# Score products of the second attention: one float32 product in place of three products of rounded halves

## The chip, the cores and the metric

The kernel runs on one core of one Trainium2 chip. The time is device time in microseconds (us) of one execution, and the figure of a kernel is the median of several executions. Engines are named as in the profile: PE is the matrix engine (PEld its weight loads), DVE the vector engine, ACT the scalar engine, POOL the general one, SP the engine that only issues transfers.

## The reference

Two layers of a decoder trunk on 256 positions of width 2048. Each layer is a token mixer and a gated ConvFFN, each followed by a residual and a layer norm, with shift, scale and gate from a conditioning vector. The mixer of layer 0 is a forgetting attention with 16 heads of width 128. The mixer of layer 1, which is the second attention, is a sliding-window attention (window 128) with 32 query heads of width 64, 4 key and value heads, and a learned sink for each head:

```
s = einsum('bnqhgd,bnkhd->bnhgqk', qb, kb) * (dh ** -0.5)     # dh = 64
p = softmax(concatenate([where(mask, s, -inf), sink], -1))[..., :-1]
o = einsum('bnhgqk,bnkhd->bnqhgd', p, vb)
```

Queries are taken in blocks of 128; a block sees its own 128 keys and the 128 before them. The first block has no keys before it. All inputs, weights and the output are float32.

## The kernel before

**Products.** PE takes float32 operands in two ways here. An operand may be rounded to the type fp32r, and a product of two such operands is one pass. To keep precision, `split` (L82) makes a rounded high half on ACT (L84) and the remainder as a low half on DVE (L85), and a product is then three: high by high, high by low, low by high. An operand left as float32 is multiplied by a plain float32 product instead; the profile shows such a product as two records of PE and two weight loads. The kernel already does so in some places: probabilities by values (`o<-pT,v` in the first attention, `o<-pT,V` in the second) and part of the first attention's output projection (`xs<-w,oW`).

**Weights.** Weights come from memory in blocks, through `stream` (L229). Each block is split by ACT (`wh`, L255) and DVE (`wl`, L259), and PE multiplies it into `ws` or `xs` banks. Of the 14,424 records of PE in the profile, those of the large projections are nearly all.

**The conditioning vectors** are sums of products on DVE (`wa`, L420), spread over the whole program at a rate that the code sets by stage.

**The second attention** is `swa` (L1042). Its input projection is taken in five blocks: keys and values first, then four blocks of queries, one for each group `g` of 8 query heads. Attention work of a group is put, step by step, between the products of later blocks: `later` (L385) queues generators, and `step` takes one step of each after a block of weights has been used. So PE's program has a piece of attention every 3 us or so, between `xs` products.

- `evac_kv` (L1051) rotates the keys on DVE, turns them on PE (`kp`), and splits the turned keys into `kT` high and low, once for each half of the positions and each pair of key heads: 4 splits in all.
- `evac_q` (L1072) scales the queries into `qb` on ACT (L1077), rotates them on DVE (L1035 to L1040), turns them on PE (`qp`, L1085), four transposes at a time, and splits the result into `qT` and `qL`: 8 splits of 128x512 in all.
- `pair` (L1092) handles two heads. The two heads lie in partitions 0 to 63 and 64 to 127 of the turned queries and of the keys (which are stored twice for that), so that the products of a pair are on two halves of the array's rows and go to two banks. For each half of the positions there are three products for each head, 12 products a pair: 6 with 128 columns and 6 with 256. Then come the masked scores and their maximum on DVE (L740), exponentials on ACT (L744), the sums on DVE (L1110 to L1114), the scaling on DVE (L1119) and ACT (L1121), the turning of the probabilities on PE (`T`, L771) with its copy on ACT (`pT`, L773), and the products by values (`o`), again for two heads at once, this time on two halves of the array's columns. There are 16 pairs.

**Order.** The order within an engine is set by the scheduling layer, from the order of the code and what depends on what; each engine then takes its instructions one after another. Tiles of a pool (`gp` has 28 buffers for `gtile`) are reused in turn.

Of the kernel before, what the change touches and what calls it, by code (L numbers as in the profile page):

```python
# [17 lines left out]
P = 128  # L18
# [8 lines left out]
SKV = 4  # L27
# [14 lines left out]
def hybrid_trunk(ctx: ExitStack, tc: tile.TileContext, a: dict, out: bass.AP):  # L42
    nc = tc.nc
    if []:
        ctx.enter_context(tc.manual_schedule(engines={getattr(mybir.EngineType, e) for e in []}))
    f32 = lambda t: t.bitcast(F32)
# [12 lines left out]
    def gtile(name="g"):  # L59
        return gp.tile([P, 2, S], F32R, tag="g", name=name)  # L60

    def ttile(name="t"):
        return tp.tile([P, 2 * S], F32, tag="t", name=name)

    def bank(name="sm"):
        return psp.tile([P, 512], F32, tag="ps", name=name)
# [7 lines left out]
    def mm(o, lhsT, rhs, start=False, stop=False, **kw):  # L74
        return nc.tensor.matmul(o, lhsT, rhs, start=start, stop=stop, **kw)  # L75
# [6 lines left out]
    def split(h, l, src):  # L82

        nc.scalar.copy(h, src)  # L84
        nc.vector.tensor_tensor(l, src, f32(h), op=ALU.subtract)  # L85
# [42 lines left out]
    for j in range(D // WB):  # L128
        ps = bank("cb")
        for i in range(WB // P):  # L130
            k = j * (WB // P) + i
            mm(ps[:, i * P:(i + 1) * P], ident[:KC, k:k + 1].broadcast_to([KC, P]), crow, start=i == 0,
               stop=i == WB // P - 1, skip_group_check=True)
# [52 lines left out]
    def then(fn):  # L186

        work.append(fn)
        if len(work) == 1 and not ahead[0]:
            settle()  # L190
# [23 lines left out]
    def defer(gen):  # L214

        post.append(gen)
# [168 lines left out]
    def later(gens, lag=1):  # L385

        bg["wait"].extend((g, lag) for g in gens)
# [346 lines left out]
    def exps(S_ps, nm, ss, nskc=None):  # L734

        pr = f32(gtile("pr")).rearrange("p a b -> p (a b)")[:, :3 * P]
        for r, (b, e) in enumerate(REGS):

            mk = mask[:, 2:3, :] if r == 0 else (mask[:, 0::2, :] if nskc is None else mask[:, 1:3, :])
            nc.vector.tensor_tensor_reduce(pr[:, b:e].rearrange("p (a k) -> p a k", k=P),  # L740
                                           S_ps[:, b:e].rearrange("p (a k) -> p a k", k=P), mk, -1.0,
                                           -NEG if nskc is None else nskc, ALU.add, ALU.min, nm[:, r:r + 1])
        for r, (b, e) in enumerate(REGS):
            nc.scalar.activation(pr[:, b:e], pr[:, b:e], AF.Exp, bias=nm[:, r:r + 1], scale=-1.0,  # L744
                                 accum_out=ss[:, r:r + 1])
        return pr
# [282 lines left out]
    def rope(t, buf, nh):  # L1029

        t1, t2, t3 = (tp.tile([P, SG, HR], F32, tag=n, bufs=1, name=n)[:, :nh, :] for n in ("r1", "r2", "r3"))
        a1, a2 = buf[:, :, 0:HR], buf[:, :, HR:2 * HR]
        cs = cost[:, t:t + 1, :].broadcast_to([P, nh, HR])
        sn = sint[:, t:t + 1, :].broadcast_to([P, nh, HR])
        nc.vector.tensor_tensor(t1, a1, sn, op=ALU.mult)  # L1035
        nc.vector.tensor_tensor(t2, a2, sn, op=ALU.mult)
        nc.vector.tensor_tensor(t3, a1, cs, op=ALU.mult)
        nc.vector.tensor_tensor(a2, a2, cs, op=ALU.mult)
        nc.vector.tensor_tensor(a1, t3, t2, op=ALU.subtract)
        nc.vector.tensor_tensor(a2, a2, t1, op=ALU.add)  # L1040

    def swa(l, j, edge, after):  # L1042
        w_in, w_o = a["swa_w_in"][j], a["swa_w_o"][j]
        KOFF = SQ * DH2
        kT = [[gtile("kT") for _ in range(SKV // 2)] for _ in range(2)]

        Vg = f32(gtile("V"))
        V = [Vg[:, t, :] for t in range(NT)]
        oT, full = {}, set()

        def evac_kv(t, ps):  # L1051
            kv = ttile("kv")
            nc.scalar.copy(kv, ps)
            kk = kv[:, 0:SKV * DH2].rearrange("p (h d) -> p h d", d=DH2)
            rope(t, kk, SKV)
            kd = ttile("kd")
            kdv = kd.rearrange("p (h u d) -> p h u d", u=2, d=DH2)
            for dup in range(2):
                nc.scalar.copy(kdv[:, :, dup, :], kk)
            yield  # L1060
            v0 = SKV * DH2
            nc.scalar.copy(V[t], kv[:, v0:])
            kp = bank("kp")
            for h in range(SKV):
                nc.tensor.transpose(kp[:, h * P:(h + 1) * P], kd[:, h * P:(h + 1) * P], ident)
            kpv = kp.rearrange("p (h s) -> p h s", s=P)
            yield
            for b in range(SKV // 2):
                split(kT[0][b][:, :, t * P:(t + 1) * P], kT[1][b][:, :, t * P:(t + 1) * P],
                      kpv[:, 2 * b:2 * b + 2, :])  # L1070

        def evac_q(g, ps):  # L1072

            qs_ = []
            for t in range(NT):
                qb = ttile("qb")
                nc.scalar.mul(qb, ps[t], DH2 ** -0.5)  # L1077
                rope(t, qb.rearrange("p (h d) -> p h d", d=DH2), SG)
                qs_.append(qb)
            yield  # L1080
            for n in range(SG // 4):
                qp = bank("qp")
                for j in range(2):
                    for t in range(NT):
                        nc.tensor.transpose(qp[:, (2 * j + t) * P:(2 * j + t + 1) * P],  # L1085
                                            qs_[t][:, (2 * n + j) * P:(2 * n + j + 1) * P], ident)
                th, tl = gtile("qT"), gtile("qL")
                split(th, tl, qp.rearrange("p (j s) -> p j s", j=2))
                later([pair(g, 2 * n + j, (th[:, j, :], tl[:, j, :])) for j in range(2)])
                yield  # L1090

        def pair(g, n, q):  # L1092
            h = g * SG + 2 * n
            qh, ql = q
            kh, kl = (kT[i][g // 2][:, g % 2, :] for i in range(2))
            rows = [slice(i * DH2, (i + 1) * DH2) for i in range(2)]
            sps = [bank("S") for _ in range(2)]
            for r in range(2):
                qs, ks = slice(r * P, (r + 1) * P), slice(0, (r + 1) * P)
                for m, (qx, kx) in enumerate(((qh, kh), (qh, kl), (ql, kh))):  # L1100
                    for o, rr in zip(sps, rows):
                        mm(o[:, r * P:(r + 1) * P + r * P], qx[rr, qs], kx[rr, ks], start=m == 0, stop=m == 2,
                           skip_group_check=True)
            yield
            nm, ss, es = (sp.tile([P, 2, 2], F32, tag=n_, name=n_) for n_ in ("nm", "ss", "es"))
            prs, pTs = [], []
            for i in range(2):
                prs.append(exps(sps[i], nm[:, i, :], ss[:, i, :], nsink[:, h + i:h + i + 1]))
                yield
            nc.vector.tensor_tensor(es, nm, sink[:, h:h + 2].rearrange("p (i o) -> p i o", o=1).broadcast_to([P, 2, 2]),  # L1110
                                    op=ALU.add)
            nc.scalar.activation(es, es, AF.Exp)
            nc.vector.tensor_tensor(ss, ss, es, op=ALU.add)
            nc.vector.reciprocal(ss, ss)  # L1114
            for i in range(2):
                for r, (b, e) in enumerate(REGS):
                    o = prs[i][:, b:e]
                    if r == 0:
                        nc.vector.tensor_scalar_mul(o, o, ss[:, i, r:r + 1])  # L1119
                    else:  # L1120
                        nc.scalar.mul(o, o, ss[:, i, r:r + 1])  # L1121
                yield
            for i in range(2):
                pTs.append(turned(prs[i]))
                yield
            ops = bank("o")
            for b, (d0, s0, s1) in enumerate(AV):
                for rr, pT in zip(rows, pTs):
                    mm(ops[rr, d0:S], V[b][:, g * DH2:(g + 1) * DH2], pT[:, s0:s1],
                       start=b == 0, stop=b == 1, skip_group_check=True)  # L1130
            kc = h // 2
            oT[kc] = o_tile(kc, ops[:, :S], l)
            full.add(kc)

        ps = head_block(w_in, KOFF, after.start)
        then(lambda: ada.update(rate=.1))
        for t in range(NT):
            then(lambda t=t, ps=ps: defer(evac_kv(t, ps[t])))
        then(lambda: (ada.update(rate=0.3), bg.update(gap=2)))
        for g in range(SKV):  # L1140
            if g == 1:
                then(lambda: ada.update(rate=0.33))
            ps = x_stationary(w_in, g * WB, 0, KC, hstat)
            then(lambda g=g, ps=ps: defer(evac_q(g, ps)))
        out_proj(oT, full, w_o, l, edge)
# [104 lines left out]
    for t in range(NT):  # L1250
        mu, rs, _ = moments[t]
# [48 lines left out]
```

## Time and profile before

| | |
|---|---|
| median of 3 executions | 2175.51 us (2174.67 to 2176.22) |
| the profiled execution | 2175.44 us |
| its span, first to last instruction | 2173.7 us |
| mean granted clock of PE | 0.997 |
| PE busy | 2131.2 us, 98% of the span |
| DVE busy | 1741.3 us, 80% |
| ACT busy | 1147.8 us, 53% |
| the second attention's pieces | from 1205 to 1384 us of the span |

The span lies 1.7 us under the execution's own time. In the profile, a product `out<-in` names the moving operand first and the weights second: `S<-kT,qL` has the keys moving over the low halves of the queries. The time of one PE record includes the way through the array, so that records overlap; the pace of PE is read from start to start.

### The profile page before, as it was taken

The numbers are of one execution on the slowest core, as the hardware profiler recorded it, in microseconds if no ns is written. First come the engines' busy times: TensorE is split into PE (matmuls) and PEld (weight loads), VectorE is DVE, ScalarE is ACT, GpSimd is POOL, SyncE is SP. The second block draws the span as 40 slices with busy tenths as digits, with TensorE's granted clock in tenths as the row PEclk, the third lists the DMA queues.
The fourth block names the chain that finished last, engine by engine and source line by source line (L and its number), as shares of the span: only waits on it lengthen the run. The fifth ranks groups of instructions, "written<-read, shape, count | busy, mean of one in ns | idle before, by whom it ended". The sixth has DMA issues, their size and how long they took to land.

```text
span 2173.7 us, 35625 instructions
## 1 busy us (share of the span) xinstructions
PE 2131.2 (98%) x14424; PEld 1917.9 (88%) x14424; DVE 1741.3 (80%) x2391; ACT 1147.8 (53%) x1782; POOL 39.3 (2%) x46
## 2 busy tenths in 40 slices
PE   6999999999999999999999999999999999999997
PEld 6999887579999888999988877789999888999986
DVE  7988898779989988988997897778888555666765
ACT  4546465255575433555555577555555633555541
POOL 1000000010000000000001000010000000000000
PEclk9999999999999999999999999999999999999999
DMA  9998988959888999888885665548777555555552
GB/s 389 420 373 304 373 332 330 369 180 353 316 297 316 337 352 356 321 330 295 323 332 223 246 252 195 184 147 310 271 272 270 194 194 194 194 194 194 194 194 96
DMA packets 89653, 598.59 MB, mean 275 GB/s; under 512 B 10016, under 2 KB 12352, under 8 KB 21136
## 3 DMA queue, kind: packets, MB, share of 16 engines
q1 hardware_dynamic: 89312, 595.87, 74.2%
q8 instruction: 113, 1.85, 0.3%
q0 software_dynamic: 176, 0.44, 0.1%
q14 instruction: 52, 0.43, 0.1%
HBM read 594.18 MB, written 2.10 MB: 274 GB/s over the span
## 4 chain that ended last, share of the span: by engine, by line
issue 56%; PE 39%; DVE 2%; DMA 2%; POOL 1%; ACT 0%; SPq 0%; DVEq 0%; ACTq 0%; POOLq 0%
PE ws L75 25%; PE xs L75 14%; DMA w<-in_fox_w_in_dram 2%; POOL x L693 0%; DVE wa L420 0%; DVE wl L259 0%; PE sm L502 0%; PE lg L75 0%; DVE x L687 0%; POOL rs L667 0%; DVE stats L661 0%; DVE x L659 0%; DVE x L1255 0%; PE sm L539 0%; DVE x L1254 0%
## 5 line engine op out<-in xcount | busy, mean ns | idle before, releaser
L255 ACT CAST wh<-w 128x1024 fp32r<-128x1024 f32 x698 | 733.2, 1053 | 727.0 <-PE ws L75 329.5
L259 DVE TENSOR_TENSOR wl<-w,wh 128x1024 fp32r<-128x1024 f32 x698 | 847.8, 1221 | 327.5 <-ACT wh L255 324.8
L75 PE MATMUL ws<-hH,wh 128*128 128x256 f32 x6400 | 1097.6, 276 | 7.4 <-ACT hH L529 6.7
L75 PEld LDWEIGHTS ws<-hH,wh 128*128 128x128 f32 x6400 | 968.5, 188 | 10.9 <-ACT hH L529 7.1
L75 PE MATMUL ws<-hH,wl 128*128 128x256 f32 x3200 | 879.9, 276 | 2.4 <-DVE wl L259 2.4
L75 PEld LDWEIGHTS ws<-hH,wl 128*128 128x128 f32 x3200 | 601.1, 188 | 3.4 <-DVE wl L259 3.3
L420 DVE CUSTOM_DVE_ANT_0 wa<-wa,cb,acol 128x2048 f32<-128x2048 f32 x192 | 449.4, 2344 | 1.0 <-DMA wa<-in_ada_w_dram 0.7
L75 PE MATMUL xs<-wh,gT 128*128 128x512 f32 x1344 | 414.7, 389 | 0.0
L75 PEld LDWEIGHTS xs<-wh,gT 128*128 128x128 f32 x1344 | 252.3, 188 | 52.3
L75 PE MATMUL xs<-wl,gT 128*128 128x512 f32 x672 | 261.4, 389 | 0.0
L75 PE MATMUL xs<-wh,hH 128*128 128x512 f32 x752 | 253.7, 402 | 3.6 <-ACT wh L255 2.9
L75 PEld LDWEIGHTS xs<-wh,hH 128*128 128x128 f32 x752 | 140.8, 189 | 36.0 <-ACT wh L255 3.5
L75 PE MATMUL xs<-wl,hH 128*128 128x512 f32 x376 | 148.8, 396 | 2.8 <-DVE wl L259 2.8
L75 PEld LDWEIGHTS xs<-wl,gT 128*128 128x128 f32 x672 | 126.2, 188 | 26.0
L1155 ACT ACTIVATE u<-ws,ccol 128x256 f32<-128x256 f32 x176 | 96.8, 562 | 52.6 <-PE ws L75 42.1
L75 PE MATMUL xs<-wh,oT 128*128 128x512 f32 x288 | 96.1, 401 | 1.1 <-ACT wh L255 1.1
L1156 DVE SCALAR_TENSOR_TENSOR u<-ws,ccol,u 128x255 f32<-128x255 f32 x176 | 82.2, 477 | 14.1 <-ACT u L1155 14.1
L75 PEld LDWEIGHTS xs<-wl,hH 128*128 128x128 f32 x376 | 71.0, 189 | 17.4 <-DVE wl L259 3.5
L1158 DVE SCALAR_TENSOR_TENSOR u<-ws,ccol,u 128x254 f32<-128x254 f32 x176 | 83.2, 476 | 2.2
L75 PEld LDWEIGHTS xs<-wh,oT 128*128 128x128 f32 x288 | 53.9, 188 | 13.2 <-ACT wh L255 1.3
L657 DVE TENSOR_TENSOR t<-xs,gate 128x512 f32<-128x512 f32 x48 | 31.5, 684 | 36.6 <-PE xs L75 36.6
L744 ACT ACTIVATE pr<-pr,nm 128x128 f32<-128x128 f32 x96 | 43.3, 452 | 32.0 <-DVE nm L740 31.8
(214 smaller groups left out, 1291.6 us busy)
## 6 DMA issues: line engine op xcount, KB each, us to landing
wa<-in_ada_w_dram SPq DMA_DIRECT2D x192, 1024.0 KB, 6.7
w<-in_ffn_w_up_dram SPq DMA_DIRECT2D x176, 1024.0 KB, 5.4
w<-in_ffn_w_down_dram SPq DMA_DIRECT2D x88, 1024.0 KB, 5.0
w<-in_fox_w_in_dram SPq DMA_DIRECT2D x60, 512.0 KB, 8.6
w<-in_swa_w_in_dram SPq DMA_DIRECT2D x20, 1024.0 KB, 5.8
w<-in_fox_w_in_dram SPq DMA_DIRECT2D x18, 1024.0 KB, 7.5
w<-in_fox_w_o_dram SPq DMA_DIRECT2D x16, 1024.0 KB, 6.9
w<-in_swa_w_o_dram SPq DMA_DIRECT2D x16, 1024.0 KB, 4.9
```

The source lines that it names most:

```text
L75: return nc.tensor.matmul(o, lhsT, rhs, start=start, stop=stop, **kw)
L255: pin(nc.scalar.copy(hp, wp_), False)
L259: nc.vector.tensor_tensor(lp, wp_, f32(hp), op=ALU.subtract)
L420: return nc.vector.tensor_tensor_reduce(w, w, cb, 1.0, acol[:, l, v * KC + k:v * KC + k + 1], ALU.mult, ALU.add, cv[:, k:k + 1])
L657: pin(nc.vector.tensor_tensor(tmp, ps[t], gate[:, d * 512:(d + 1) * 512], op=ALU.mult), end)
L744: nc.scalar.activation(pr[:, b:e], pr[:, b:e], AF.Exp, bias=nm[:, r:r + 1], scale=-1.0, accum_out=ss[:, r:r + 1])
L1155: nc.scalar.activation(u, pf, AF.Identity, bias=cw(CW, f), scale=cw(2, f))
L1156: nc.vector.scalar_tensor_tensor(u[:, 1:], pf[:, :S - 1], cw(1, f), u[:, 1:], op0=ALU.mult, op1=ALU.add)
L1158: nc.vector.scalar_tensor_tensor(u[:, 2:], pf[:, :S - 2], cw(0, f), u[:, 2:], op0=ALU.mult, op1=ALU.add)
```

## The change

The turned keys are copied to one float32 tile for each pair of key heads (2 tiles in place of 4), the turned queries to one float32 tile (in place of `qT` and `qL`), both by a copy on ACT. Each score product is one float32 product. A pair then issues 4 products (2 with 128 columns, 2 with 256) in place of 12.

```diff
-        kT = [[gtile("kT") for _ in range(SKV // 2)] for _ in range(2)]
+        kT = [f32(gtile("kT")) for _ in range(SKV // 2)]
...
             for b in range(SKV // 2):
-                split(kT[0][b][:, :, t * P:(t + 1) * P], kT[1][b][:, :, t * P:(t + 1) * P],
-                      kpv[:, 2 * b:2 * b + 2, :])
+                nc.scalar.copy(kT[b][:, :, t * P:(t + 1) * P], kpv[:, 2 * b:2 * b + 2, :])
...
-                th, tl = gtile("qT"), gtile("qL")
-                split(th, tl, qp.rearrange("p (j s) -> p j s", j=2))
-                later([pair(g, 2 * n + j, (th[:, j, :], tl[:, j, :])) for j in range(2)])
+                qT = f32(gtile("qT"))
+                nc.scalar.copy(qT, qp.rearrange("p (j s) -> p j s", j=2))
+                later([pair(g, 2 * n + j, qT[:, j, :]) for j in range(2)])
...
-            qh, ql = q
-            kh, kl = (kT[i][g // 2][:, g % 2, :] for i in range(2))
+            k = kT[g // 2][:, g % 2, :]
...
-                for m, (qx, kx) in enumerate(((qh, kh), (qh, kl), (ql, kh))):
-                    for o, rr in zip(sps, rows):
-                        mm(o[:, r * P:(r + 1) * P + r * P], qx[rr, qs], kx[rr, ks], start=m == 0, stop=m == 2,
-                           skip_group_check=True)
+                for o, rr in zip(sps, rows):
+                    mm(o[:, r * P:(r + 1) * P + r * P], q[rr, qs], k[rr, ks], start=True, stop=True,
+                       skip_group_check=True)
```

Lines behind the change lie up to three lower in the changed kernel (L1113 becomes L1110, L1119 becomes L1116).

On PE, the first pair (and the `xs` products and query transposes `qp` around it) stands so before:

```order
L75 MATMUL xs<-wl,hH 128x512
L75 MATMUL xs<-wh,hH 128x512
L75 MATMUL S<-kT,qT 128x128 x4
L75 MATMUL S<-kT,qL 128x128 x2
L75 MATMUL S<-kT,qT 128x256 x4
L75 MATMUL S<-kT,qL 128x256 x2
L1085 MATMUL qp<-ident,qb 128x128 x4
```

and so in the changed kernel:

```order
L75 MATMUL xs<-wl,hH 128x512
L75 MATMUL xs<-wh,hH 128x512
L75 MATMUL S<-kT,qT 128x128 x2
L75 MATMUL S<-kT,qT 128x256 x2
L1084 MATMUL qp<-ident,qb 128x128 x4
```

The place among the other products is the same, for all 16 pairs; only the rows of a pair become fewer.

On DVE, at the second pair of the second group (masked scores L740, sums, and the scaling of the probabilities), the order before is:

```order
L740 ISA pr,nm<-S,mask,nsink 128x256
L740 ISA nm 128x1
L1113 TENSOR_TENSOR ss<-ss,es 128x4
L259 TENSOR_TENSOR wl<-w,wh 128x1024
L1114 RECIPROCAL ss<-ss 128x4
L85 TENSOR_TENSOR qL<-qp,qT 128x512
L1119 TENSOR_SCALAR pr<-pr,ss 128x128 x2
L740 ISA pr,nm<-S,mask,nsink 128x128
```

and in the changed kernel:

```order
L740 ISA pr,nm<-S,mask,nsink 128x256
L740 ISA nm 128x1
L1110 TENSOR_TENSOR ss<-ss,es 128x4
L259 TENSOR_TENSOR wl<-w,wh 128x1024
L1111 RECIPROCAL ss<-ss 128x4
L259 TENSOR_TENSOR wl<-w,wh 128x1024
L1116 TENSOR_SCALAR pr<-pr,ss 128x128 x2
L740 ISA pr,nm<-S,mask,nsink 128x128
```

The subtraction `qL` is gone, and a later `wl` subtraction has moved to its place, ahead of the scaling of the probabilities.

## The prediction

> **What bounds the kernel now.** I read the page's table of engines first, then PE's own waits while the second attention runs, then the table by stretches of that stage.
>
> ```profile
> PE 2131.2 (98%) x14424; PEld 1917.9 (88%) x14424; DVE 1741.3 (80%) x2391; ACT 1147.8 (53%) x1782; POOL 39.3 (2%) x46
> ...
> PE S L75 <- DVE qL L85: 2.1, 2, 1.2
> PE qp L1085 <- DVE qb L1040: 1.3, 2, 0.8
> ...
> 1230.00:1265.00 35.00, 33.71 (x191) 26.40 (x190) 34.65 (x85) 23.32 (x51) 0.00 (x0) 1.00 0.73 268
> 1265.00:1300.00 35.00, 33.76 (x209) 25.72 (x208) 29.74 (x91) 26.86 (x71) 0.00 (x0) 1.00 0.68 240
> 1335.00:1370.00 35.00, 34.10 (x206) 25.81 (x205) 25.34 (x78) 25.28 (x69) 0.00 (x0) 1.00 0.47 166
> ```
>
> PE sets the time. In the stretches (width, then busy time of PE, PEld, DVE, ACT, POOL, then clock) PE stands still for 1.3, 1.2 and 0.9 us, at granted clock 1.00. All its waits are on DVE: for low halves of the queries, which the change abolishes, and for rotated queries (`qb`), late because DVE is full (34.65 of 35 us). So two things count: what a pair's scores take on PE, and which waits end.
>
> **The products of a pair.** PE and its weight loads at an undisturbed pair, and PE at a group of products by values:
>
> ```profile
> 1256.34 0.44 PE L75 MATMUL S<-kT,qT 64*128 64x128 f32 x4
> 1256.73 0.45 PE L75 MATMUL S<-kT,qT 64*128 64x256 f32 x4
> 1257.22 0.50 PE L75 MATMUL xs<-wh,hH 128*128 128x512 f32 x1
> ...
> 1256.34 0.30 PEld L75 LDWEIGHTS S<-kT,qT 64*128 64x128 f32 x4 [0.17 <-issue]
> ...
> 1256.90 0.19 PEld L75 LDWEIGHTS S<-kT,qL 64*128 64x128 f32 x2
> ...
> 1260.21 0.87 PE L75 MATMUL o<-pT,V 128*64 128x256 f32 x8
> 1261.01 0.55 PE L771 MATMUL T<-ident,pr 128*128 128x128 f32 x3
> ...
> 369.93 3.60 PE L75 MATMUL xs<-w,oW 128*128 128x512 f32 x8
> 373.36 0.49 PE L771 MATMUL T<-ident,pr 128*128 128x128 f32 x3
> ...
> 1259.66 0.39 PE L75 MATMUL xs<-wl,hH 128*128 128x512 f32 x1
> 1259.89 0.39 PE L75 MATMUL xs<-wh,hH 128*128 128x512 f32 x1
> ```
>
> A pair takes 1257.22 - 1256.34 = 0.88 us from its start to the next work. Its 12 loads go in twos, one for each head (four of them, two such steps, are busy for 0.30, one step and a load of 0.19), the first at 1256.34, the last two at 1256.90. Five steps take 0.56 us, 0.11 each, and the 128-column products (1256.34 to 1256.73 for three steps) keep the same step. So the weight loads pace the group, more than the columns.
>
> A float32 product: eight records with 512 columns take 373.36 - 369.93 = 3.43 us, 0.43 each, and two records make a product, 0.86; a rounded product takes 0.23 (1259.66 to 1259.89). A record moves 512 columns in 0.43, so 256 in 0.215 and 128 in 0.107. A new pair has two records for 128 and two for 256 columns in each head: 2 x 0.107 + 2 x 0.215 = 0.64 us if the two heads run together, as they do now, and 1.29 if one after another. The nearest row is the group by values: the same columns, 2 x (128 + 256) in float32 on two halves of the array. It takes 1261.01 - 1260.21 = 0.80 us, so its halves do run together, with 0.16 for start and end. Its weights have 64 columns, a score's 128. Only the first load lies bare; at 0.11 for 128 columns, 64 more cost 0.055. The rest lie under records of 0.107 or longer. So a pair takes 0.80 + 0.055 = 0.855 us: 16 x (0.855 - 0.88) = **-0.4 us**. Its ends: 0.80 (-1.3 in all), and both heads one after another, 1.29 + 0.16 + 0.055 = 1.50 (+9.9). I take the value near the group by values, a row of float32 halves run together.
>
> The Trainium skill, "FP8 and Floating Point Precision", section TensorE Precision Notes, counts true float32 as four passes through the array, against three for the products removed. The trace agrees on the four (0.86 against 0.23 is 3.7). By passes alone the change would cost PE time; that sum is a rival below, from the rows.
>
> **The waits.** The disturbed places, and an undisturbed one of the query transposes to set against them:
>
> ```profile
> 1266.70 0.44 PE L75 MATMUL S<-kT,qT 64*128 64x128 f32 x4
> 1268.37 0.33 PE L75 MATMUL S<-kT,qL 64*128 64x128 f32 x2 [1.24 <-DVE qL L85]
> 1269.03 0.66 PE L1085 MATMUL qp<-ident,qb 128*128 128x128 f32 x4
> ...
> 1335.75 0.68 PE L75 MATMUL S<-kT,qT 64*128 64x128 f32 x4
> 1337.27 0.33 PE L75 MATMUL S<-kT,qL 64*128 64x128 f32 x2 [0.84 <-DVE qL L85]
> 1337.93 0.66 PE L1085 MATMUL qp<-ident,qb 128*128 128x128 f32 x4
> ...
> 1353.89 0.82 PE L75 MATMUL S<-kT,qT 64*128 64x128 f32 x4
> 1355.16 0.50 PE L75 MATMUL xs<-wh,oT 128*128 128x512 f32 x1
> ...
> 1262.37 0.30 PE L1085 MATMUL qp<-ident,qb 128*128 128x128 f32 x1 [0.81 <-DVE qb L1040]
> 1263.45 0.48 PE L75 MATMUL xs<-wh,hH 128*128 128x512 f32 x1
> ...
> 1297.95 0.55 PE L771 MATMUL T<-ident,pr 128*128 128x128 f32 x3
> 1298.69 0.48 PE L75 MATMUL xs<-wh,hH 128*128 128x512 f32 x1
> ...
> 1234.69 0.68 DVE L85 TENSOR_TENSOR qL<-qp,qT 128x512 fp32r<-128x512 f32 x1
> 1235.29 0.68 DVE L712 SCALAR_TENSOR_TENSOR x<-x,ln 128x512 f32<-128x512 f32 x1
> ...
> 1263.73 0.59 ACT L84 CAST qT<-qp 128x512 fp32r<-128x512 f32 x1
> 1334.89 0.59 ACT L84 CAST qT<-qp 128x512 fp32r<-128x512 f32 x1
> ```
>
> Two pairs stop in their middle for `qL`: 2.33 us (1266.70 to 1269.03) and 2.18 (1335.75 to 1337.93), against 0.88. That is 1.45 + 1.30 = 2.75 us. Their high halves had been ready: `qT` ended at 1264.32 and 1335.48, ahead of the pairs' starts, and the changed pair waits for that copy alone. So **-2.75**. A third pair loses 1.27 - 0.88 = 0.39 (1353.89 to 1355.16) with no `qL` named; I leave it as it is (0), its end is -0.39.
>
> The query transposes from 1262.37 wait for the rotation. From the `T` products at 1261.01 to the next `xs` at 1263.45 are 2.44 us; the same work takes 0.74 at 1297.95. That is 1.70 lost. DVE works without a pause before it, and one `qL` there costs it 0.60 (1234.69 to 1235.29); two lie between 1230 and 1262. So the rotation ends 1.20 earlier, and 0.50 of the wait stays: **-1.20**, with ends 0 and -1.70.
>
> **What may come back.** DVE's order has a `wl` subtraction where `qL` stood, ahead of the scaling. ACT scales the other part of the same probabilities just before `T`:
>
> ```profile
> 1288.96 0.91 ACT L1121 ACTIVATE pr<-pr,ss 128x256 f32<-128x256 f32 x2 [0.50 <-DVE ss L1114]
> 1289.70 0.55 PE L771 MATMUL T<-ident,pr 128*128 128x128 f32 x3
> ...
> L420 DVE CUSTOM_DVE_ANT_0 wa<-wa,cb,acol 128x2048 f32<-128x2048 f32 x12 | 28.1, 2345 | 0.0
> L85 DVE TENSOR_TENSOR qL<-qp,qT 128x512 fp32r<-128x512 f32 x8 | 5.5, 683 | 0.0
> L85 DVE TENSOR_TENSOR kT<-kp,kT 128x256 fp32r<-128x256 f32 x4 | 1.5, 418 | 0.1
> L84 ACT CAST qT<-qp 128x512 fp32r<-128x512 f32 x8 | 4.6, 579 | 0.4 <-PE qp L1085 0.4
> L447 ACT COPY gate<-sm 128x512 f32<-128x512 f32 x2 | 1.2, 586 | 0.0
> ```
>
> The two scalings at 1288.96 take 0.91, the first half of that, to 1289.42; `T` starts at 1289.70, 0.28 later. A PE that comes 3 or 4 us earlier can meet these chains unfinished. The chains also begin on PE and move with it, so most of the gain stays. I allow **+1.0** for new waits, between 0 and 2.34 (one `wa` sum put ahead of a scaling).
>
> At nothing: DVE loses 5.5 + 1.5 = 7.0 us of subtractions, under PE's work apart from the waits counted. ACT's float32 copies cost what its roundings cost (586 against 579 ns for 128x512), on an engine with a third of each stretch idle. Transfers and POOL keep their order. Freed buffers cost nothing, and no wait of PE here names one. If PE's cover went, these 7 us would be a gain that I don't count.
>
> **Sum.** -0.4 - 2.75 - 1.20 + 1.0 = -3.35 us. The span 2173.7 becomes 2170.3; the profiled execution lies 1.74 above its span (2175.44) and 0.07 under the median, so the median becomes 2175.51 - 3.35 = **2172.2 us**, 0.15% less.
>
> **Rivals.**
>
> A. Forecast: heads together, the `qL` waits gone, some waits back: 2172.2, of its own range 2169.4 (-1.3 - 2.75 - 1.70 - 0.39 = -6.1) to 2173.9. Chance 0.66.
>
> B. Slower: float32 products on two halves of the array's rows don't run together. For it: no row here shows float32 on row halves, the group by values uses column halves. Against: rounded products do run together on row halves, and float32 ones on column halves. Price 16 x (1.50 - 0.88) = +9.9, so 2175.51 + 9.9 - 2.75 - 1.20 + 1.0 = 2182.5. It decides once a pair takes over 0.88 + 2.95 / 16 = 1.06 us. Chance 0.12. The Trainium skill, "TensorE: Matmul & The Clock Gate", section Part 3: Packing small matmuls, has products in distinct row groups start some 4 ns apart, naming no type; no run here shows it for float32.
>
> C. The passes decide. Three rounded products of 512 columns take 3 x 0.23 = 0.69, one float32 product 0.86; on a pair's 384 columns the difference is 0.17 x 384 / 512 = 0.13 us, 16 times +2.0 instead of -0.4: 2174.6. Against it, the pair's loads now pace it at 0.11 a step where 128 columns need 0.23 / 4 = 0.06. Chance 0.06.
>
> D. The waits move and don't end: the scaling of the probabilities, behind `wl` and `wa`, stops PE for as long as `qL` did. Then -0.4 alone, 2175.1. For it, 0.28 us of slack at `T`; against it, DVE has 7 us less to do. Chance 0.16.
>
> **How the numbers follow.** The time is A's, 2172.2. The range takes A's lower end and D, and leaves out B: 2169.3 to 2176.0. What a measurement of this kernel can tell from no change is about 0.2%, 4.35 us, so the border is 2171.2. A lies below it with 0.29 of its 0.66 (where less of the waits comes back than allowed): faster 0.29. No change has the other 0.37 of A, C's 0.06 and 0.14 of D: 0.57. Slower has B's 0.12 and 0.02 of D, where more comes back than was gained.
>
> **What would show it.** Right: an undisturbed pair takes 0.85 us with 8 records, the two heads' records starting together; no wait of PE names `qL` or a query copy; the wait of `qp` on `qb` near 1262 shrinks to half a microsecond; DVE's busy time falls by 7 us. Wrong: records of a pair one after another (1.5 us, B), a step that follows the passes (1.0 us, C), or waits of `T`, `qp` or `o` on L1116, L1118 or L1040 that sum to over 2.3 us (D).

## The result and the profile after

The changed kernel takes 2170.15 us, the median of 11 runs, ten of which lie between 2169.84 and 2171.52. The kernel before took 2175.89 beside it (11 runs, 2174.67 to 2177.55). The ratio is 0.9974, with a 95% interval from 0.9966 to 0.9982: 0.26%, or 5.7 us, faster. One of the 11 runs (2374.68 us) and one of ten of the first experiment below (3588.45 us) went at a lower granted clock, 0.851 and 0.558; they move the medians by at most 0.2 us and do not enter the ratios. The prediction was 2172.2 us, 0.15% faster, with "no change" as its likeliest outcome.

The profiled execution of the changed kernel took 2171.03 us, its span 2169.2 (before: 2175.44 and 2173.7). The table of engines:

```profile
PE 2129.6 (98%) x14360; PEld 1914.5 (88%) x14360; DVE 1735.5 (80%) x2379; ACT 1148.8 (53%) x1782; POOL 39.3 (2%) x46
```

PE has 64 records fewer: 16 pairs with 8 in place of 12. PE still sets the time. What changed is how long it stands still in the second attention. The table by stretches (start and end, width, then busy time of PE, PEld, DVE, ACT, POOL, then granted clock, share of the transfers and GB/s), first of the kernel before for the whole stage, which the prediction did not show:

```profile
1205.00:1400.00 195.00, 191.57 (x1079) 149.22 (x1078) 160.47 (x405) 131.41 (x308) 0.00 (x0) 1.00 0.60 213
```

and of the changed kernel, with the same three shorter stretches as in the prediction:

```profile
1230.00:1265.00 35.00, 34.96 (x182) 26.73 (x182) 34.77 (x91) 23.93 (x51) 0.00 (x0) 1.00 0.77 285
1265.00:1300.00 35.00, 35.00 (x205) 26.09 (x205) 31.98 (x98) 27.95 (x76) 0.00 (x0) 1.00 0.71 263
1335.00:1370.00 35.00, 35.00 (x196) 25.88 (x195) 21.08 (x66) 26.00 (x68) 0.00 (x0) 1.00 0.38 136
1205.00:1400.00 195.00, 194.96 (x1039) 149.67 (x1038) 159.30 (x397) 136.71 (x314) 0.00 (x0) 1.00 0.60 222
```

PE's idle time in these 195 us falls from 195 - 191.57 = 3.43 us to 0.04. The list of PE's waits in the stage, two rows before, is empty now. Note that DVE is as full as it was from 1230 to 1265 (34.77 of 35 us): it did not become free, it was merely no longer late at the places where PE needs it.

The pairs and the query transposes on PE in the changed kernel (start, duration, engine, line, operation, count). The first three rows are an undisturbed place; the next are the place of the wait on rotated queries, the two places where a pair stopped for `qL`, and the third disturbed pair:

```profile
1256.79 0.49 PE L771 MATMUL T<-ident,pr 128*128 128x128 f32 x3
1257.21 0.93 PE L75 MATMUL S<-kT,qT 64*128 64x128 f32 x8
1258.06 0.50 PE L75 MATMUL xs<-wh,hH 128*128 128x512 f32 x1
...
1261.81 0.55 PE L771 MATMUL T<-ident,pr 128*128 128x128 f32 x3
1262.19 0.86 PE L1084 MATMUL qp<-ident,qb 128*128 128x128 f32 x4
1262.81 0.48 PE L75 MATMUL xs<-wh,hH 128*128 128x512 f32 x1
...
1266.09 0.93 PE L75 MATMUL S<-kT,qT 64*128 64x128 f32 x8
1266.94 0.66 PE L1084 MATMUL qp<-ident,qb 128*128 128x128 f32 x4
...
1333.17 0.93 PE L75 MATMUL S<-kT,qT 64*128 64x128 f32 x8
1334.02 0.66 PE L1084 MATMUL qp<-ident,qb 128*128 128x128 f32 x4
...
1349.92 0.93 PE L75 MATMUL S<-kT,qT 64*128 64x128 f32 x8
1350.78 0.50 PE L75 MATMUL xs<-wh,oT 128*128 128x512 f32 x1
```

A pair takes 0.85 to 0.86 us from its start to the next work wherever it stands: 1257.21 to 1258.06, 1266.09 to 1266.94, 1333.17 to 1334.02, 1349.92 to 1350.78. (The starts without rounding give 0.855 to 0.857 for all 16; I use 0.856.) The three pairs that took 2.33, 2.18 and 1.27 take that too. In the pair at 1257.21 the records of the two heads start 7 ns apart, four times over (3 to 6 ns for the rounded products before, at 1256.34). From the `T` products to the next `xs`, the place that took 2.44 us takes 1.00 (1261.81 to 1262.81).

Now the stage as a whole. These are the first key transposes and the last pair with the work after it, in the kernel before:

```profile
L1065 PE MATMUL kp<-ident,kd x8: 271/272/276, 1209.6 to 1210.4; 128*128 128x128 f32 x8
...
1362.53 0.44 PE L75 MATMUL S<-kT,qT 64*128 64x128 f32 x4
```

and in the changed kernel:

```profile
L1065 PE MATMUL kp<-ident,kd x8: 271/273/276, 1210.6 to 1211.3; 128*128 128x128 f32 x8
...
1358.11 0.93 PE L75 MATMUL S<-kT,qT 64*128 64x128 f32 x8
```

From the first key transpose to the start of the last pair are 152.9 us before (1209.6 to 1362.53) and 147.5 after (1210.6 to 1358.11): 5.4 us less. What follows the last pair takes as long as before (798.7 and 798.6 us to PE's last record). The span is only 4.5 us shorter, because the changed kernel reached the stage 1.0 us later, through code that the change does not touch. The first 100 us of each, before and after:

```profile
0.00:100.00 100.00, 82.45 (x527) 75.77 (x528) 81.36 (x76) 49.05 (x67) 5.78 (x24) 0.98 0.99 403
```

```profile
0.00:100.00 100.00, 82.10 (x523) 75.53 (x524) 80.51 (x76) 49.17 (x67) 5.78 (x24) 0.93 0.99 401
```

The granted clock was 0.98 in the one execution and 0.93 in the other. That belongs to the execution and not to the kernel, as the last section shows. The medians over many runs differ by 5.7 us, the stage by 5.4.

### The profile page after: what moved, and what is told of

It reads as the page before. It is cut to its first block, busy times and chain, and to the rows that moved or that the text cites. A ratio compares the mean times of both kernels' runs of the same rounds, so it can differ in the third digit from the quotient of the medians.

```text
span 2169.2 us, 35481 instructions
## 1 busy us (share of the span) xinstructions
PE 2129.6 (98%) x14360; PEld 1914.5 (88%) x14360; DVE 1735.5 (80%) x2379; ACT 1148.8 (53%) x1782; POOL 39.3 (2%) x46
## 4 chain that ended last, share of the span: by engine, by line
issue 56%; PE 40%; DVE 2%; DMA 1%; POOL 1%; ACT 0%; SPq 0%; DVEq 0%; ACTq 0%; POOLq 0%
PE ws L75 25%; PE xs L75 14%; DMA w<-in_fox_w_in_dram 1%; DVE wa L420 1%; POOL x L693 0%; DVE wl L259 0%; PE sm L502 0%; PE lg L75 0%; DVE x L687 0%; POOL rs L667 0%; DVE stats L661 0%; DVE x L659 0%; DVE x L1252 0%; PE sm L539 0%; DVE x L1251 0%
```

## The experiments

Two questions were open. First, what was the loss: the waits for the subtractions (PE standing in the middle of a pair), the load of the subtractions on DVE, or the products themselves? Second, why does a float32 pair take 0.856 us: do the heads run together whatever the order of the program, and what sets the pace?

**Is it DVE's load?** This kernel is the changed one with the 12 subtractions put back on DVE; nothing reads their results.

```diff
         kT = [f32(gtile("kT")) for _ in range(SKV // 2)]
+        kL = [gtile("kL") for _ in range(SKV // 2)]
...
+                nc.vector.tensor_tensor(kL[b][:, :, t * P:(t + 1) * P], kpv[:, 2 * b:2 * b + 2, :], hi, op=ALU.subtract)
...
+                nc.vector.tensor_tensor(gtile("qL"), qp.rearrange("p (j s) -> p j s", j=2), qT, op=ALU.subtract)
```

> The changed kernel, with the 12 subtractions of the low halves put back on DVE (8 of 128x512, 4 of 128x256, 7 us in all); nothing reads their results, so PE waits for none of them. Theory W (PE lost its time where it waited for the low halves themselves): the two waits of 1.45 and 1.30 us stay away, a pair takes 0.86 us, and the time is 2175.9 - 0.5 - 2.75 = 2172.6 us or less; the wait of the query transposes for the rotated queries near 1262 us, 1.70 us, is back because DVE is as full as before. Theory L (DVE's load is what held PE up, wherever it was waited for): nearly all waits are back in other places, time 2175 us.

Measured: 2170.85 us, ratio 0.9977 (0.9968 to 0.9987). The subtractions run, and PE has one wait left in the stage:

```profile
L1091 DVE TENSOR_TENSOR qL<-qp,qT x8: 681/684/691, 1235.5 to 1335.7; 128x512 fp32r<-128x512 f32 x8
```

```profile
PE qp L1087 <- DVE qb L1040: 0.4, 1, 0.4
```

All 16 pairs stay at 0.856 us. So DVE can carry the 7.0 us of subtractions (8 x 0.684 and four of the keys) at a price of 0.4 us in the stage (147.9 us from the first key transpose to the start of the last pair, 147.5 in the changed kernel). In the medians it is 0.7 us, less than the width of the interval, and nearly all of the gain stays. The loss was that PE waited for the subtractions, not that DVE made them. The wait on the rotated queries does come back, as the prediction's step for it says, but at 0.4 us and not at 1.70: in this kernel the scheduling has put two `xs` products between `T` and the query transposes and three more behind the first of these, and they cover a part of it. So this run bounds that step and does not measure it.

**Is it the products?** Rounded products again, three for each score, but with no low halves: the queries and keys are rounded once, and the high product is summed three times. The corrections are left out and the scores are three times too large; time alone is read from it.

```diff
-                qT = f32(gtile("qT"))
+                qT = gtile("qT")
...
-                for o, rr in zip(sps, rows):
-                    mm(..., start=True, stop=True, ...)
+                for m in range(3):
+                    for o, rr in zip(sps, rows):
+                        mm(..., start=m == 0, stop=m == 2, ...)
```

> Queries and keys rounded once on ACT, no low halves, and the same high product taken three times, so that PE has the 12 rounded products of the kernel before and DVE no subtraction; the corrections by the low halves are left out. Theory W (the gain comes from waits and DVE's load, the form of the product is worth 16 x 0.03 us): a pair takes 0.88 us, no wait in the stage, time 2170.15 + 0.5 = 2170.6 us. Theory P (the gain comes from the form of the product on PE): nearer to the kernel before, 2174 us or more.

Measured: 2173.47 us, ratio 0.999 (0.9981 to 0.9999), between the two expectations. Undisturbed pairs take 0.88 us, as before the change. But the waits list has two new rows:

```profile
PE S L75 <- DVE oT L85: 1.0, 1, 1.0
PE S L75 <- ACT qT L1087: 0.6, 1, 0.6
```

The first of them on PE, and what DVE did just then:

```profile
1265.32 0.32 PE L75 MATMUL S<-kT,qT 64*128 64x128 f32 x1
1266.63 0.95 PE L75 MATMUL S<-kT,qT 64*128 64x128 f32 x11 [0.99 <-DVE oT L85]
1267.52 0.66 PE L1084 MATMUL qp<-ident,qb 128*128 128x128 f32 x4
...
1263.89 2.35 DVE L259 TENSOR_TENSOR wl<-w,wh 128x1024 fp32r<-128x1024 f32 x2
1266.16 0.41 DVE L85 TENSOR_TENSOR oT<-o,oT 128x256 fp32r<-128x256 f32 x1
```

The scheduling has put two `wl` subtractions (2.35 us) ahead of `oT`, and the pair's second product, the first of the other head, does not start until `oT` has read its source. This pair takes 2.20 us (1265.32 to 1267.52) in place of 0.88. The second row is a wait for a copy of the queries on ACT: from the `T` products at 1300.02 to the pair at 1301.14 are 1.12 us, in the changed kernel 0.42 (1299.21 to 1299.63), so 0.7 is lost. With 16 x (0.88 - 0.856) = 0.4, that is 1.32 + 0.7 + 0.4 = 2.4 of the 2.8 us by which the stage is longer than the changed kernel's. So the run does not separate the two theories cleanly: low halves gone, it still lost PE's time to waits, but to other ones. It shows instead that a new wait of the kind the prediction allowed for (a `wl` or `wa` put ahead of something PE needs) is real; with the other one it costs 2.0 us, within the 0 to 2.34 that were allowed. Such waits come with one order and not with another; the changed kernel's order had none.

**Does the order of the heads matter?** The changed kernel with both products of the first head, then both of the second:

```diff
-            for r in range(2):
-                qs, ks = ...
-                for o, rr in zip(sps, rows):
+            for o, rr in zip(sps, rows):
+                for r in range(2):
+                    qs, ks = ...
```

> The changed kernel with the four products of a pair in another order: both products of the first head, then both of the second, in place of the heads in turn. Orders of the other engines stay. Theory O (PE starts products in the order of its program, and two row halves run together only where products of the two heads alternate): the two heads run nearly one after another, a pair takes 1.3 to 1.5 us in place of 0.86, 16 x 0.45 to 0.65 = 7 to 10 us more, 2177 to 2180 us. Theory I (each half of the rows takes its own products as they come): 0.86 us a pair, 2170.2 us.

Measured: 2170.42 us, ratio 0.9978 (0.9969 to 0.9986). The first pair and the work after it:

```profile
1237.04 0.93 PE L75 MATMUL S<-kT,qT 64*128 64x128 f32 x8
1237.91 0.66 PE L1084 MATMUL qp<-ident,qb 128*128 128x128 f32 x4
```

A pair takes 0.87 us (0.863 without rounding). The two heads run together although the program asks for them one after the other; the theory that the alternation makes them overlap would have cost 7 to 10 us, and falls. The trace shows when records start and not in which order they were issued. That the order did change is read from the edit and from the second head's records, which now start 13 or 14 ns behind the first's in place of 7.

**What is a product worth?** One rounded product for each score (corrections left out, so the scores carry the rounding of queries and keys):

```diff
-                qT = f32(gtile("qT"))
+                qT = gtile("qT")
```

> Queries and keys rounded once, and one rounded product of the high halves for each score block: the corrections by the low halves are left out. PE then has 4 products of one record a pair. By the pace of the weight loads (0.11 us a step, the first one bare) a pair takes 0.16 + 0.11 + 0.10 = 0.37 us in place of 0.86. Theory W with PE as the bound: 16 x 0.49 = 7.8 us less than the changed kernel, 2162.3 us, if the scheduling layer makes no new wait; up to 2165.5 us with waits like the 1.3 and 0.9 us that the run with three high products had. If the engines beside PE set the pace of the stage, most of it is lost: 2168 us or more.

Measured: 2163.66 us, ratio 0.9943 (0.9929 to 0.9956).

```profile
1234.69 0.50 PE L75 MATMUL S<-kT,qT 64*128 64x128 f32 x4
1235.12 0.66 PE L1084 MATMUL qp<-ident,qb 128*128 128x128 f32 x4
```

A pair takes 0.43 us, half a float32 pair's 0.856 and half of the three rounded products' 0.88. So 16 x 0.43 = 6.9 us of PE's work are gone, and the median is 6.7 us under the changed kernel's in the same comparison (2170.4): in this stage PE's time counts one to one. The number also fits a simple account of a pair, though none of its parts was varied alone: four loads take two steps, 0.22 us at 0.11; the other 0.21 are start and end; twelve loads take six steps, 0.66, and again 0.22. The float32 pair fits it by its columns, 0.64, and again 0.22; its eight loads, four steps, would need only 0.44. I expected 0.37 here: start and end were taken too small.

**Was it the place of the wait in the pair?** The kernel before, with the low-by-high products behind all the others. DVE and ACT do the same in the same order. This order does not give the right scores; the products are the same ones, and time alone is read from it.

```diff
-            for r in range(2):
-                qs, ks = ...
-                for m, (qx, kx) in enumerate(((qh, kh), (qh, kl), (ql, kh))):
+            for m, (qx, kx) in enumerate(((qh, kh), (qh, kl), (ql, kh))):
+                for r in range(2):
+                    qs, ks = ...
```

> The kernel before, with a pair's products in another order: high by high and high by low for both halves of the positions first, then low by high for both. The orders of DVE and ACT stay as before. If the two long pairs stop for the low half of the queries, the stop now lies behind eight products in place of four and the pairs take about 2.15 and 2.0 us in place of 2.34 and 2.18, the others 0.88, and the third one, 1.27 us, which names no low half, stays. If they stopped for something else that these products share, the stop stays where it was, behind the first products. 2175 us, no difference that can be timed.

Measured: 2175.03 us in a single run, in the middle of the runs of the kernel before (2174.74 to 2177.54). The three disturbed pairs:

```profile
1266.36 0.72 PE L75 MATMUL S<-kT,qT 64*128 64x128 f32 x8
1268.04 0.50 PE L75 MATMUL S<-kT,qL 64*128 64x128 f32 x4 [0.95 <-DVE qL L85]
1268.46 0.66 PE L1085 MATMUL qp<-ident,qb 128*128 128x128 f32 x4
...
1335.17 1.17 PE L75 MATMUL S<-kT,qT 64*128 64x128 f32 x8
1336.88 0.50 PE L75 MATMUL S<-kT,qL 64*128 64x128 f32 x4 [0.55 <-DVE qL L85]
1337.31 0.66 PE L1085 MATMUL qp<-ident,qb 128*128 128x128 f32 x4
...
1353.24 0.32 PE L75 MATMUL S<-kT,qT 64*128 64x128 f32 x1
1353.89 0.72 PE L75 MATMUL S<-kT,qT 64*128 64x128 f32 x7 [0.33 <-DVE nm L740]
...
1354.78 0.50 PE L75 MATMUL xs<-wh,oT 128*128 128x512 f32 x1
```

The stop moves behind the eight products that need only the high half. From the start of the low-by-high products to the next work are now 0.42 us (1268.04 to 1268.46) and 0.43 (1336.88 to 1337.31); from the same stop it was 0.66 in both pairs before (1268.37 to 1269.03, 1337.27 to 1337.93). The first pair shrinks with that, to 2.10 us in place of 2.33. The second stays near its length (2.14 in place of 2.18), because PE comes to it earlier against DVE: its first eight products now wait 0.26 us on the weight loads for `oT`, a wait that was 0.2 before. The stops follow the low half wherever it is used, so they are waits for `qL` and not for a bank or a weight load.

The third pair is another matter: its stop names the scores of an earlier pair (`nm`, L740) and no low half. I had expected it to stay at 1.27 us; it took 1.54 (1353.24 to 1354.78). Two more pairs, at 1318.11 and 1326.38, took 0.95 and 1.05 with no wait of PE named, which was not expected and is not explained.

**Does the same change pay in the first attention?** There each score sums a rounded product of `A` and `Bm` and three rounded products of queries and keys. The three become one float32 product, beside the same change in the second attention:

```diff
-                th, tl = gtile("qh"), gtile("ql")
+                th = f32(gtile("qh"))
...
-                    split(th, tl, src)
+                    nc.scalar.copy(th, src)
...
-                    mm(o, qh[:, qs], kh[:, ks], skip_group_check=True)
-                    mm(o, qh[:, qs], kl[:, ks], skip_group_check=True)
-                    mm(o, ql[:, qs], kh[:, ks], stop=True, skip_group_check=True)
+                    mm(o, qh[:, qs], kh[:, ks], stop=True, skip_group_check=True)
```

> The changed kernel with the same change in the first attention: turned queries and keys unrounded, one float32 product beside the rounded product that carries the forget terms. DVE loses 32 subtractions there. On PE a head has 2 rounded products and 2 float32 products of two records in place of 8 rounded products; at 0.11 us for a rounded one with its load and 0.107 and 0.215 for a record of 128 and 256 columns that is 2 x 0.11 + 0.64 = 0.86 against 8 x 0.11 = 0.88 us, no difference. Theory W: only waits for these halves can be won, and PE names none of them there, so 2169 to 2170.2 us. Theory L (less load on DVE is worth time where DVE is full): DVE is busy for 259 of 300 us there, 20 us of its work go, and PE's 7 us of idle time in that stretch shrink by some us: 2166 us.

> The change in both attentions once more: 2168.6 us as before, 1.6 us under the changed kernel, if the gain is one of the program and not of one chip; 2170 us if it was chance.

> The changed kernel once more, beside the next one on the same chip: 2170.2 us, 0.9974 of the kernel before.

Measured: 2168.58 us, ratio 0.9965 (0.9953 to 0.9978), and on another chip 2167.09, ratio 0.996 (0.9948 to 0.9973). There the changed kernel itself had 2170.4, ratio 0.9974 (0.9964 to 0.9985). So it is 1.6 and 3.3 us under the changed kernel; the intervals overlap, but it came out under it both times, and it has the lowest medians of the kernels here that drop no correction. One head's scores and the products after it:

```profile
204.39 0.22 PE L75 MATMUL S<-Bm,A 128*128 128x128 f32 x1
...
204.85 0.59 PE L75 MATMUL S<-qh 128*128 128x256 f32 x2
205.09 0.59 PE L75 MATMUL ws<-hH,wh 128*128 128x256 f32 x2
205.51 0.29 PE L75 MATMUL ws<-hH,wl 128*128 128x256 f32 x1
```

The group itself takes 205.09 - 204.39 = 0.70 us in place of 0.91, but the first two `ws` products behind it then take 0.42 (205.09 to 205.51) in place of 0.23: the end of the float32 products lies inside the next work. Group and delay together cost some 0.9 us against 0.91, no real difference. What this stage gained, 2.6 us between the first score and the key transposes of the second attention (1009.15 to 1006.54 us), therefore comes from elsewhere. DVE's busy time in 100 to 400 us fell from 258.95 to 251.18 us, but PE's named waits from 190 to 420 us fell only from 6.9 to 6.1 us, so they hold 0.8 of it. Where the rest comes from stays open. I had expected 20 us off DVE there and got 7.8: there are 16 such subtractions and not 32, at 0.68 us.

## Why the prediction was right, and where not

The direction, the place and the mechanism were right. The gain was put at 3.35 us and came as 5.7, and the outcome called likeliest, "no change", was not the one that came.

**The products of a pair** (0.855 us, -0.4): measured 0.856. The step that took a float32 group on column halves as the row for float32 on row halves, and added half a weight load, held; that it met the time to a nanosecond is luck, since its rows are read to 10 ns. Rival B (heads one after another, 1.50 us) falls: the heads' records start 7 ns apart. The Trainium skill, "TensorE: Matmul & The Clock Gate", section Part 3: Packing small matmuls, says some 4 ns for products in distinct row groups; this trace has 7 for float32. Rival C (1.01 us, by passes) falls too. One float32 product in place of three rounded ones does cost more columns' time; but the old pair was paced by its twelve loads, six steps of 0.11 us, and not by its passes, as the pair of one rounded product confirms: with two of three products gone it is 0.45 us shorter, which is four steps of 0.11, while their columns, at 0.23 for 512, need 0.35.

**The two `qL` waits** (-2.75): both gone, and the pairs at these places take 0.86, so 1.47 + 1.32 = 2.79. The kernel with the unread subtractions shows that it was the waiting: DVE with the same 7 us of work cost the stage 0.4 us.

**The third pair** (0, end -0.39): it went too, 1.27 - 0.86 = 0.41. With the low halves last, its stop is put down to the scores of an earlier pair, and in the kernel before its weight loads wait for the same (0.4 us for `nm`, L740); it is a wait of its own, which did not recur at the new times. Leaving it at 0 was one of the sizes that were too small.

**The query transposes** (-1.20, 0.50 to stay): 2.44 became 1.00 us, so -1.44, and 1.00 - 0.74 = 0.26 stays (the weight loads of these transposes still wait 0.28 us for `qb`). The rotation ended earlier against the `T` products than two subtractions of 0.60 explain. The prediction left out that the four subtractions of the keys (1.5 us, at the start of the stage) lie ahead of it as well. The rotation ended 53.5 us after the first key transpose in the kernel before, 51.9 in the changed one, and 53.4 in the one with all twelve subtractions back and unread, so the subtractions together are nearly all of it. How much of that is the keys' was not tried alone.

**New waits** (+1.0, ends 0 and 2.34): none. This is the step that failed, and the largest part of the miss. PE's waits in the stage are empty. The prediction read its slack of 0.28 us at a place (`T` at 1289.70) where the order of DVE did not change. The one scaling that got a `wl` ahead of it which was not there before is at another place, and there the `T` products come late:

```profile
1267.01 1.20 DVE L259 TENSOR_TENSOR wl<-w,wh 128x1024 fp32r<-128x1024 f32 x1
1268.12 0.48 DVE L1116 TENSOR_SCALAR pr<-pr,ss 128x128 f32<-128x128 f32 x2
...
1271.07 0.55 PE L771 MATMUL T<-ident,pr 128*128 128x128 f32 x3
```

The scaling ends at 1268.60, and `T` starts 2.47 us later: a `wl` of 1.20 us is hidden there. The idea of new waits was sound, as three rounded products without low halves show: there the order put two `wl` ahead of `oT` and PE stood for 1.0 us. But which order comes cannot be read from the slack of another place. The order of the changed kernel was at hand, and the prediction charged a general allowance where it could have followed the moved `wl` to the start of what stood behind it.

**The sum.** Thirteen undisturbed pairs at 0.88 - 0.856 give 0.3; with 2.79, 0.41 and 1.44 that is 4.9 of the 5.4 us that the stage lost. The remaining 0.4 us or so is spread between the pairs, where the `xs` products follow each other a few ns closer: from the transposes behind the disturbed pair to the next pair are 7.74 us before (1269.03 to 1276.78) and 7.71 after (1266.94 to 1274.65), and so on from pair to pair. Its cause was not looked for. Without the allowance the prediction's own terms give -4.35, 2171.2, and with the third pair 2170.8.

**DVE's busy time** falls by 5.8 us (1741.3 to 1735.5), not by 7.0. The removed rows do sum to 7.0, but each overlaps its neighbours: the first `qL` is 0.68 us long and the next row starts 0.60 after it. Busy time counts an overlap once; without the twelve rows the trace of the kernel before has DVE busy for 1735.7 us. Rival D (waits move) had its condition tested by the waits list and falls for this order.

**The chances.** The border of "faster" lay at 2171.2, in the middle of the forecast's own range. The +1.0 moved the forecast across it; with the allowance at nothing the forecast would have stood on the border, and with the third pair below it. One end of that range does not add up: 2169.4 is the sum of the lower ends, but the upper ends (0 for the query transposes, 2.34 for new waits) sum to 2174.7 and not to 2173.9. The outcome does not hang on it.

## What to carry to other kernels

Where PE sets the time and is 98% busy, look for the few groups of products that take longer than their like: here three of 16 pairs and one group of transposes held 4.6 us, while the shorter score products themselves were worth 0.4. A split of an operand puts a subtraction of another engine into the chain of a product; dropping it paid here where PE waited, for the remainder itself (2.8 us) or for a rotation that stood behind it (1.4 us); the same 7 us of subtractions that nothing waited for cost the stage 0.4. And count a group of small products by its weight loads as well as its columns: three rounded products and one float32 product of 128 to 256 columns took the same time within 3%.

## What the runs showed of the hardware that was not expected

Float32 products on two halves of the array's rows run together in both orders that were tried: a pair takes 0.856 us with the heads alternating in the program and 0.863 head by head.

The end of a float32 group can reach into the work behind it. In the first attention the group grew shorter by 0.21 us, and the products behind it longer by 0.19, so a group's own time from first start to next start is not its price.

The clock of the opening differs between executions of one kernel. The kernel with the change in both attentions, profiled twice, on two chips, first 100 us of each and then its key transposes:

```profile
0.00:100.00 100.00, 83.50 (x527) 76.40 (x528) 81.35 (x76) 49.05 (x67) 5.78 (x24) 0.97 0.99 403
...
L1061 PE MATMUL kp<-ident,kd x8: 271/272/276, 1207.2 to 1207.9; 128*128 128x128 f32 x8
```

```profile
0.00:100.00 100.00, 81.69 (x518) 75.05 (x519) 79.98 (x74) 48.34 (x66) 5.78 (x24) 0.93 0.99 396
...
L1061 PE MATMUL kp<-ident,kd x8: 271/273/276, 1208.9 to 1209.7; 128*128 128x128 f32 x8
```

With a granted clock of 0.93 in place of 0.97 in the first 100 us, the second attention starts 1.7 us later, in the same kernel. It does not take another chip for that: the second one's five runs show mean clocks of 0.995 (2169.37 us, the one profiled) and 0.997 to 0.998 (2166.35 to 2167.37). A single profiled execution can therefore be off by more than a term of such a sum, and stages should be measured from a landmark of their own.
